# A one-layer decoder kernel: x on one DMA queue, and another order of work around the first products

## The chip, the cores and the metric

The kernel runs on one core of a Trainium2 chip. The metric is the device time of one execution in microseconds (us). A core has a matrix engine (PE, whose weight loads the profile lists as PEld), VectorE (DVE), ScalarE (ACT), GpSimd (POOL) and SyncE (SP), each with its own instruction stream; SP, ACT and POOL can issue DMA transfers. PE reads its operands from SBUF and writes into eight banks of PSUM.

## The reference

One layer of a decoder, batch 1, 512 tokens, width 1024, all in float32. What matters here is how it opens: a conditioning vector c gives a modulation (shift and scale, one row of weights for each), x is normalised and modulated, and multiplied by a wide input matrix.

```python
def layer(x, c, positions, ...):
    mod = silu(c) @ w_ada + b_ada               # shift, scale and gate of both sub-layers
    h   = rmsnorm(x, g1) * (1 + scale1) + shift1
    z   = h @ w_in                              # q, f, i, g of HGRN2; q, k, v, gates of NSA
    o   = concat(hgrn2(z...), nsa(z..., positions)) @ w_out
    x   = x + gate1 * o
    ...                                         # a second sub-layer: gated MLP with a causal convolution
```

The attention heads use rotary embeddings (sines and cosines of the positions), the recurrence uses a lower bound on its gate; both need small tables made from the inputs.

## The kernel before

**Precision.** Products of float32 values are made of three products in a reduced form: an operand is split into a high part (a cast, on ACT) and a low part (a subtraction, mostly on DVE), and high by high, high by low and low by high are summed in PSUM (`mm3`, `split`; lines L145, L146, L149 to L151).

**The opening.** x comes as four tiles of 128 tokens by 1024. For each, ACT squares and sums (`x_square`, L515), DVE and POOL make the inverse root (`x_rstd`, L349 and L350), DVE scales the tile (`x_scale`, L521), PE transposes it ("flips", `xn_flip`, L358: eight blocks of 128x128 a tile, four a half), and ACT or DVE copies the flipped blocks out of PSUM into `xnT` (`xn_out`, L363). The feature axis is cut into eight groups of 128, the turns k = 0 to 7. For each turn the modulation needs one shift and one scale column. For k = 0, 1, 2, 3 and 5 (`PROWS`) a row of products on PE makes it (`ada_first_row`, L376; its copy from PSUM by ACT is L381), then two transposes turn it into columns (`ada_cols`, L394, reduced on DVE in L395). For k = 4, 6 and 7 DVE sums the row (`sums_first`, L605 and L607) and PE adds up over partitions (L402). `h_scale` (L405, L406) makes `sh` and `a` of a column. The turn's input is `hT` = a * xnT + sh, in two parts: for k = 0 `h_first` (L413 to L416), for the others ACT makes the high part and the full value (L627) and DVE the low part (L634).

**The products.** A turn has three groups of four products on `accq` (L658: hT high by w high, hT high by w low, hT low by w high) and two triples on `accf` (L149 to L151). `wq` and `wf` are the split weights, from the raw tiles `raw` and `rawf`. The accumulators share PSUM banks with the tiles `ps` into which x is flipped.

**The tables.** `tables` makes, in small pieces, the gate's constants (`identr`, `onesr`, `bsc`, `lbv`, `fc`; L428 to L435), and the angles of the rotary embedding (L449 to L468).

**Order.** Up to the first products the order in which each engine works is the order in which the code is written. From there it is a string, `OPEN`: each letter takes one step of a part: P a group of products, R half a row on PE, s one sum on DVE, c a column, h a high part, l a low part, w a split of `wq`, f a split of `wf`, d the next load, t a piece of the tables, k a piece of later weights. A step that needs another forces it to be taken first (`reach`): P asks for `hT`'s low part and the weights of its turn, h for the column, c for the row. Within an engine nothing overtakes.

**Loads.** SP issues nearly all of them in the order of `LOADS`: the modulation's weights `ada` (two halves of 512 KB for each turn), `raw` (256 KB a turn) and `rawf`, behind the tiles of x, `vrow` (rows of small inputs) and `grow` (gains of heads). Tiles 1 and 2 of x and the constants `cb` are issued by ACT. Each SP transfer also waits for the landing of one that was issued eight transfers before it.

Of the kernel before, what the change touches and what calls it, by code (L numbers as in the profile page):

```python
# [10 lines left out]
F32R = mybir.dt.float32r  # L11
# [4 lines left out]
ALU = mybir.AluOpType  # L16
# [3 lines left out]
P = 128  # L20
# [8 lines left out]
HD = 64  # L29
# [2 lines left out]
WARM2 = 6  # L32
NPE = 3
AHD = 3
WARM4 = 4
PGP = 0
FLU = 1
FO = 1
# [7 lines left out]
GROUPS = tuple((k,) for k in range(8))  # L46
LOADS = "aqfaqcaaqfqaqaqfaifqaq"
PROWS = (0, 1, 2, 3, 5)
OPEN = ("tRwRPdPPcRRPPtRhcRhlRRPlfddPsdddcdPdwPddsPPPwshssdPPPdtdlPPPsddcwtddRfsdPhPssslcRwdhRPPsssPlsPsPPcfP",
        "sPsPhssssPsPwlcRhPPPtssPtPkwPtlPPPt")  # L50
EPOS = 1
VLAG = 1
# [52 lines left out]
def hybrid_layer_kernel(ctx: ExitStack, tc: tile.TileContext, d: dict, out: bass.AP, dbg=None):  # L105
    nc = tc.nc
    ve, sc, gp, pe, sp = nc.vector, nc.scalar, nc.gpsimd, nc.tensor, nc.sync
# [33 lines left out]
    def f32(ap):  # L141
        return ap.bitcast(F32)
# [20 lines left out]
    x_view = d["x"].rearrange("b (i p) c -> p (b i) c", p=P)  # L163
# [117 lines left out]
    xs = []  # L281
    for i in range(NT):
        xi = G([D], s="x")
        (sc if i in (1, 2) else sp).dma_start(xi, x_view[:, i, :])
        xs.append(xi)
        if i == 0:
            vrow = cst.tile([R_ALL, P], F32, name="vrow")
            sp.dma_start(vrow, d["rows"])
            grow = cst.tile([1, 4 * HD], F32, name="grow")
            sp.dma_start(grow, d["head_gains"])  # L290

    raw_f = []
    raw_q = []
# [17 lines left out]
    gains = cst.tile([P, 4, HD], F32, name="gains")  # L311
# [21 lines left out]
    ones = cst.tile([P, P], F32, name="ones")  # L333
# [20 lines left out]
    def xn_flip(i, half):  # L354
        ps = PS()
        for k in range(4):
            kk = half * 4 + k
            pe.transpose(ps[:, k * P:(k + 1) * P], xs[i][:, kk * P:(kk + 1) * P], ident)  # L358
        return ps.rearrange("p (e k t) -> p e k t", e=2, k=2)

    def xn_out(i, half, copy, ps, es=(0, 1)):
        for e in es:
            copy(xnT[2 * half + e][:, :, i * P:(i + 1) * P], ps[:, e])  # L363
# [23 lines left out]
    def ada_cols(g):  # L387
        t, one = arow.pop(g)
        m = len(GROUPS[g])
        if one is sel:  # L390
            c0 = 0 if m > 1 else 256 * (g % 2)
            turned = adcs[0][:, c0:c0 + m * 256]
            for b in range(2 * m):
                pe.transpose(turned[:, b * P:b * P + P], t[:, b % 2, b // 2 * P:b // 2 * P + P], ident)  # L394
            ve.tensor_reduce(acol[:, 2 * GROUPS[g][0]:2 * GROUPS[g][0] + 2 * m],  # L395
                             turned.rearrange("p (e g w) -> p e g w", e=2 * m, g=4)[:, :, :, 0], AX.X, ALU.add)
            ready[g] = acol
            return
        ready[g] = adcs[0]
        for n, k in enumerate(GROUPS[g]):  # L400
            for e in range(2):
                pe.matmul(adcs[0][:, 2 * k + e:2 * k + e + 1], t[:, e, n * P:(n + 1) * P], one, start=True, stop=True)  # L402

    def h_scale(k, adc):
        ve.tensor_tensor(sh1[:, k:k + 1], adc[:, 0:1], vt[:, k:k + 1], ALU.add)  # L405
        ve.scalar_tensor_tensor(a1[:, k:k + 1], adc[:, 1:2], bsc1[:, k:k + 1], vt[:, 48 + k:49 + k],  # L406
                                ALU.add, ALU.mult)

    def h_first(w):

        h = G([2, T], F32R, s="hT")
        t = TMP([P, T], tag="ht")
        ve.tensor_scalar(h[:, 0], xnT[0][:, 0], a1[:, 0:1], sh1[:, 0:1], ALU.mult, ALU.add)  # L413
        sc.activation(t, xnT[0][:, 0], AF.Identity, bias=sh1[:, 0:1], scale=a1[:, 0:1])
        ve.tensor_tensor(w[:, 1], raw_q[0], f32(w[:, 0]), ALU.subtract)
        ve.tensor_tensor(h[:, 1], t, f32(h[:, 0]), ALU.subtract)  # L416
        hT.append(h)
# [80 lines left out]
    def first_gates(k, eng):  # L498
        w = G([2, 2, 256], F32R, s="wf")
        split(w[:, 0], w[:, 1], raw_f[k // 2], eng)  # L500
        return w

    def warm_up(n):

        for _ in range(n):
            pe.matmul(warm, wrm[:, 0:P], wrm, start=True, stop=True)
# [6 lines left out]
    def x_square(i):  # L513
        sq = TMP([P, D], BF16, tag="sq")
        sc.activation(sq, xs[i], AF.Square, accum_out=ss1[:, i:i + 1])  # L515

    def x_rstd(i):
        rstd(rs1[:, i:i + 1], ss1[:, i:i + 1], 1.0 / D, EPS)

    def x_scale(i):  # L520
        ve.tensor_scalar(xs[i], xs[i], rs1[:, i:i + 1], None, ALU.mult)  # L521

    vps, gps = PS(), PS()
# [9 lines left out]
    pe.transpose(vps[:, 0:R_ALL], vrow, ident[0:R_ALL, 0:R_ALL])  # L533
    for _ in range(WARM2):
        pe.matmul(warm, wrm[:, 0:P], wrm, start=True, stop=True)
    sc.activation(csig, vps[:, R_C:R_C + KT], AF.Tanh, scale=0.5)
    x_rstd(0)
    ve.tensor_copy(vt, vps[:, 0:R_ALL])
    ve.tensor_scalar(bsc1, vt[:, 8:16], 1.0, None, ALU.add)
    x_scale(0)  # L540
    x_square(1)
    fl = {}
    for half in range(2):
        fl[0, half] = xn_flip(0, half)
    x_rstd(1)
    ve.scalar_tensor_tensor(cs, csig, 1.0, vt[:, R_C:R_C + KT], ALU.add, ALU.mult)
    ve.tensor_scalar(cs, cs, 0.5, None, ALU.mult)
    ve.tensor_copy(cs32, cs.unsqueeze(2).to_broadcast([P, KT, 32]))
    x_square(2)
    x_scale(1)  # L550
    x_rstd(2)
    for half in range(2):
        fl[1, half] = xn_flip(1, half)
    pe.matmul(gps[:, 0:4 * HD], ones[0:1], grow, start=True, stop=True)
    xn_out(0, 0, ve.tensor_copy, fl[0, 0])
    x_square(3)
    x_scale(2)
    xn_out(0, 1, sc.copy, fl[0, 1])
    xn_out(1, 0, sc.copy, fl[1, 0])
    for half in range(2):  # L560
        fl[2, half] = xn_flip(2, half)
    x_rstd(3)
    x_scale(3)
    for _ in ada_first_row(0):
        pass
    xn_out(2, 0, ve.tensor_copy, fl[2, 0])
    fl[3, 0] = xn_flip(3, 0)
    ada_cols(0)
    adc = ready[0][:, 0:2]
    xn_out(3, 0, ve.tensor_copy, fl[3, 0], (0,))  # L570
    fl[3, 1] = xn_flip(3, 1)
    w = G([2, 512], F32R, s="wq")
    sc.copy(w[:, 0], raw_q[0])
    h_scale(0, adc)
    h_first(w)
    xn_out(3, 0, ve.tensor_copy, fl[3, 0], (1,))
    xn_out(1, 1, sc.copy, fl[1, 1])
    xn_out(2, 1, sc.copy, fl[2, 1])
    xn_out(3, 1, sc.copy, fl[3, 1])
    ve.tensor_scalar(gains[:, 0], gps[:, 0:HD], HD ** -0.5, None, ALU.mult)  # L580
    ve.tensor_copy(gains[:, 1:4], gps[:, HD:4 * HD].rearrange("p (g c) -> p g c", g=3))
    wfk = first_gates(0, None)
    warm_up(WARM4)
    qw, fw = [w], [wfk]
    last = {}

# [95 lines left out]
    def advance(letter):  # L682
        name = same.get(letter, letter)
        last[name] = letter
        if next(opening[name], opening) is opening:
            return False
        made[name] += 1
        return True

    def reach(name, n):  # L690
        while made[name] < n:
            assert advance(name), name

# [1302 lines left out]
```

## Time and profile before

| | us |
|---|---|
| median of three runs | 678.23 (677.64 to 680.0) |
| the profiled execution | 678.53 |
| its span, first to last instruction | 676.7 |
| mean granted clock of PE | 0.999 |
| PE busy | 665.1 (98%) |
| DVE busy | 497.8 (74%) |
| ACT busy | 354.3 (52%) |
| POOL busy | 183.5 (27%) |

A row of the timeline gives the start, the busy time of the group, the engine, the line, the operation, the output and inputs, how many instructions, and in brackets how long the engine was idle ahead of it and what ended that. A row of stages gives the window and its length, the busy time and the number of instructions of PE, PEld, DVE, ACT and POOL, the granted clock of PE, the busy share of the DMA engines and their rate. Instructions on one engine overlap a little, so starts lie closer together than durations. Times are from the start of the span.

### The profile page before, as it was taken

What the parts mean: (1) busy time and instruction counts of PE and PEld (TensorE: products, weight loads), DVE (VectorE), ACT (ScalarE), POOL (GpSimd) and SP (SyncE); (2) the same over time, 40 slices, a digit from 0 to 9 for tenths busy, and PEclk for the clock granted to TensorE, in tenths of its full rate; (3) what the DMA queues carried; (4) which work ended last, traced back from release to release, by engine and by line L of the source; (5) the groups of instructions that cost most, each with busy time, mean ns of one, the idle gap of its engine ahead of it and who ended that gap; (6) DMA issues with size and microseconds to landing.
All of it is one profiled execution on the core that took longest, in us unless ns stands there. A gap on an engine that the chain in (4) does not pass through costs nothing.

```text
span 676.7 us, 11052 instructions
## 1 busy us (share of the span) xinstructions
PE 665.1 (98%) x4147; PEld 550.6 (81%) x4148; DVE 497.8 (74%) x971; ACT 354.3 (52%) x658; POOL 183.5 (27%) x185
## 2 busy tenths in 40 slices
PE   8999999999999999999999999999999999999996
PEld 4778898788888888888988888888888888888885
DVE  5788988979899879688746556655656558676997
ACT  5756447756687778245543434544433436464551
POOL 1006111000010100100036666747758645000000
PEclk9999999999999999999999999999999999999999
DMA  9936364576122316152258889999988946974662
GB/s 337 411 142 204 95 201 130 184 235 219 55 72 87 133 37 239 39 183 61 73 153 243 219 234 266 241 280 300 236 234 222 262 106 222 334 264 164 224 273 93
DMA packets 100731, 130.43 MB, mean 193 GB/s; under 512 B 6380, under 2 KB 67653, under 8 KB 100679
## 3 DMA queue, kind: packets, MB, share of 16 engines
q1 hardware_dynamic: 95735, 117.09, 51.4%
q0 software_dynamic: 4512, 11.54, 9.5%
q10 hardware_dynamic: 432, 1.12, 0.4%
q8 instruction: 32, 0.52, 0.3%
q14 instruction: 20, 0.16, 0.1%
HBM read 123.29 MB, written 29.50 MB: 226 GB/s over the span
## 4 chain that ended last, share of the span: by engine, by line
PE 81%; DVE 10%; ACT 5%; DMA 2%; issue 1%; ACTq 0%; SPq 0%; DVEq 0%
PE u L150 12%; PE u L149 12%; PE u L151 12%; PE dn L149 5%; PE dn L150 5%; PE dn L151 5%; PE accq L658 3%; PE oh L149 2%; PE oh L151 2%; PE oh L150 2%; PE oT L1127 2%; PE F L1098 2%; PE pT L149 2%; PE pT L151 2%; PE pT L150 2%
## 5 line engine op out<-in xcount | busy, mean ns | idle before, releaser
L146 DVE TENSOR_TENSOR wlo<-raw,whi 128x1024 fp32r<-128x1024 f32 (+1 forms) x67 | 90.9, 1358 | 100.5 <-ACT whi L145 100.4
L149 PE MATMUL u<-h2h,whi 128*128 128x512 f32 (+1 forms) x360 | 136.8, 380 | 0.0
L150 PE MATMUL u<-h2l,whi 128*128 128x512 f32 (+1 forms) x360 | 136.7, 380 | 0.0
L151 PE MATMUL u<-h2h,wlo 128*128 128x512 f32 (+1 forms) x360 | 136.7, 380 | 0.0
L145 ACT CAST whi<-raw 128x1024 fp32r<-128x1024 f32 (+1 forms) x67 | 68.8, 1028 | 80.9 <-PE u L150 74.3
L149 PEld LDWEIGHTS u<-h2h,whi 128*128 128x128 f32 x360 | 67.7, 188 | 12.9
L151 PEld LDWEIGHTS u<-h2h,wlo 128*128 128x128 f32 x360 | 67.7, 188 | 12.8
L150 PEld LDWEIGHTS u<-h2l,whi 128*128 128x128 f32 x360 | 67.7, 188 | 12.7
L350 POOL TENSOR_TENSOR hrs<-hrs,mhalf 128x4 f32<-128x4 f32 (+2 forms) x16 | 18.6, 1173 | 90.7 <-DVE hrs L349 88.7
L145 ACT CAST whi<-wd 128x1024 fp32r<-128x1024 f32 x20 | 21.1, 1055 | 40.5 <-PE dn L151 33.4
L1734 ACT ACTIVATE y<-y 128x512 f32<-128x512 f32 x22 | 13.9, 632 | 52.1 <-DVE y L1731 52.0
L1065 ACT ACTIVATE pt<-pt,mx 128x128 f32<-128x128 f32 (+3 forms) x64 | 35.9, 564 | 9.2 <-DVE mx L1049 8.1
L149 PE MATMUL pT<-hT,whi 128*128 128x512 f32 x96 | 38.3, 399 | 0.0
L150 PE MATMUL pT<-hT,whi 128*128 128x512 f32 x96 | 37.6, 391 | 0.0
L151 PE MATMUL pT<-hT,wlo 128*128 128x512 f32 x96 | 37.5, 391 | 0.0
L146 DVE TENSOR_TENSOR wlo<-wd,whi 128x1024 fp32r<-128x1024 f32 x20 | 25.5, 1275 | 14.3 <-ACT whi L145 14.3
L1730 DVE SCALAR_TENSOR_TENSOR y<-u,cv,y 128x511 f32<-128x511 f32 x44 | 32.6, 740 | 2.9 <-ACT y L1729 2.9
L150 PE MATMUL dn<-wlo,as 128*128 128x512 f32 x88 | 34.4, 391 | 0.1
L151 PE MATMUL dn<-whi,as 128*128 128x512 f32 x88 | 34.3, 389 | 0.0
L149 PE MATMUL dn<-whi,as 128*128 128x512 f32 x88 | 34.2, 389 | 0.0
L1731 DVE SCALAR_TENSOR_TENSOR y<-u,cv,y 128x510 f32<-128x510 f32 x44 | 32.9, 749 | 1.6
L1729 ACT ACTIVATE y<-u,cv 128x512 f32<-128x512 f32 x44 | 34.0, 773 | 0.0
(364 smaller groups left out, 1600.8 us busy)
## 6 DMA issues: line engine op xcount, KB each, us to landing
raw<-in_w_up SPq DMA_DIRECT2D x44, 512.0 KB, 6.1
aw<-in_w_ada SPq DMA_DIRECT2D x24, 512.0 KB, 4.0
ada<-in_ada_first SPq DMA_DIRECT2D x16, 512.0 KB, 8.1
raw<-in_w_in SPq DMA_DIRECT2D x7, 1024.0 KB, 5.1
wt<-in_w_down POOLq DMA_DIRECT2D x11, 512.0 KB, 8.6
wd<-in_w_down SPq DMA_DIRECT2D x11, 512.0 KB, 5.8
wt<-in_w_down SPq DMA_DIRECT2D x10, 512.0 KB, 6.5
wt<-in_w_down POOLq DMA_DIRECT2D x5, 1024.0 KB, 11.7
```

The costliest lines, as they stand in the source:

```text
L145: sc.copy(hi, src)
L146: (eng or ve).tensor_tensor(lo, src, f32(hi), ALU.subtract)
L149: pe.matmul(o, ah, bh, start=start, stop=False, skip_group_check=True)
L150: pe.matmul(o, ah, bl, start=False, stop=False, skip_group_check=True)
L151: pe.matmul(o, al, bh, start=False, stop=stop, skip_group_check=True)
L350: gp.tensor_tensor(o, o, mhalf[:, 0:n], ALU.pow)
L658: pe.matmul(accq[i], h[:, e, i * P:(i + 1) * P], w[:, f], start=(k + e + f == 0), stop=(e == 1 and k == KT - 1), skip_group_check=True)
L1065: sc.activation(pt[:, sl], pt[:, sl], AF.Exp, bias=mx[:, e:e + 1], scale=-1.0, accum_out=su[:, h % 2, e:e + 1])
L1729: sc.activation(y, u, AF.Identity, bias=cv[:, 132 + c:133 + c], scale=cv[:, 88 + c:89 + c])
L1730: ve.scalar_tensor_tensor(y[:, 1:], u[:, :T - 1], cv[:, 44 + c:45 + c], y[:, 1:], ALU.mult, ALU.add)
L1731: ve.scalar_tensor_tensor(y[:, 2:], u[:, :T - 2], cv[:, c:c + 1], y[:, 2:], ALU.mult, ALU.add)
L1734: sc.activation(y, y, AF.Silu)
```

## The change

All of it lies in the opening, about the first 30 us.

- All four tiles of x are issued by SP; `grow` goes to ACT's queue.
- The body up to the first products is written in another order: the squares of tiles 1 to 3 stand ahead of other work, the inverse roots of tiles 2 and 3 ahead of the scaling of tile 2; the gains are made early; the copies of tile 0 are all ACT's; row 0 of the modulation stands ahead of the flips of tile 2.
- Only the first half of tiles 2 and 3 is flipped ahead of the first products. The second halves follow the first group of products (`advance("P")`).
- The high part of turn 0's `wq` is cast by POOL in place of ACT.
- Five warm-up products in place of four, now ahead of `h_first`.
- `OPEN` has another first part: row 1 stands behind the first products, and the tables' pieces (t) behind the low part of turn 2.

```diff
-WARM4 = 4
+WARM4 = 5
-OPEN = ("tRwRPdPPcRRPPtRhcRhlRRPlfddPsdddcdPdwPddsPPPwshssd...
+OPEN = ("wPRRRPcPPhlPRRRPchPltRRRPPtfddsdddcddwddsPPwshssd...
-        (sc if i in (1, 2) else sp).dma_start(xi, x_view[:, i, :])
+        sp.dma_start(xi, x_view[:, i, :])
-            sp.dma_start(grow, d["head_gains"])
+            sc.dma_start(grow, d["head_gains"])
...
     for _ in ada_first_row(0):
         pass
-    xn_out(2, 0, ve.tensor_copy, fl[2, 0])
-    fl[3, 0] = xn_flip(3, 0)
+    w = G([2, 512], F32R, s="wq")
+    gp.tensor_copy(w[:, 0], raw_q[0])
+    xn_out(0, 1, sc.copy, fl[0, 1])
+    fl[2, 0] = xn_flip(2, 0)
+    xn_out(2, 0, ve.tensor_copy, fl[2, 0], (0,))
     ada_cols(0)
-    adc = ready[0][:, 0:2]
+    fl[3, 0] = xn_flip(3, 0)
     xn_out(3, 0, ve.tensor_copy, fl[3, 0], (0,))
-    fl[3, 1] = xn_flip(3, 1)
-    w = G([2, 512], F32R, s="wq")
-    sc.copy(w[:, 0], raw_q[0])
+    adc = ready[0][:, 0:2]
     h_scale(0, adc)
-    h_first(w)
-    xn_out(3, 0, ve.tensor_copy, fl[3, 0], (1,))
+    warm_up(WARM4)
     xn_out(1, 1, sc.copy, fl[1, 1])
-    xn_out(2, 1, sc.copy, fl[2, 1])
-    xn_out(3, 1, sc.copy, fl[3, 1])
+    h_first(w)
+    for i in (2, 3):
+        xn_out(i, 0, sc.copy, fl[i, 0], (1,))
...
+    advance("P")
+    for i in (2, 3):
+        fl[i, 1] = xn_flip(i, 1)
+        xn_out(i, 1, sc.copy, fl[i, 1])
     for row in OPEN:
```

Behind the edits the code's lines are three lower: L627 becomes L624, L634 L631, L658 L655, L605 L602, L607 L604; from the 700s on they are one higher.

On SP's queue before, with the names of the tiles (x_79, x_85, x_87 and x_89 are tiles 0 to 3):

```order
1 L284 DMA x_79<-in_x 128x1024
2 L288 DMA vrow<-in_rows 112x128
3 L290 DMA grow<-in_head_gains 1x256
4 L284 DMA x_89<-in_x 128x1024
5 L277 DMA ada_93<-in_ada_first 128x1024
6 L277 DMA ada_95<-in_ada_first 128x1024
```

and now:

```order
1 L284 DMA x_79<-in_x 128x1024
2 L288 DMA vrow<-in_rows 112x128
3 L284 DMA x_85<-in_x 128x1024
4 L284 DMA x_87<-in_x 128x1024
5 L284 DMA x_89<-in_x 128x1024
6 L277 DMA ada_93<-in_ada_first 128x1024
```

Tiles 1 and 2 now stand ahead of tile 3 and of the modulation's weights in one queue.

On PE before, from row 0 of the modulation to the first products (ps are flipped halves of x, adc the column, wrm the warm-up):

```order
41 L376 MATMUL warm_110<-ada_93,cs_157 32x256 x4
42 L376 MATMUL warm_110<-ada_95,cs_157 32x256 x4
43 L358 MATMUL ps_247<-cb,x_89 128x128 x4
44 L394 MATMUL adc_152<-cb,row_243 128x128 x2
45 L358 MATMUL ps_256<-cb,x_89 128x128 x4
```

and now, with the second halves of tiles 2 and 3 behind the first group of products:

```order
39 L376 MATMUL warm_110<-ada_93,cs_157 32x256 x4
40 L376 MATMUL warm_110<-ada_95,cs_157 32x256 x4
41 L358 MATMUL ps_239<-cb,x_87 128x128 x4
42 L394 MATMUL adc_152<-cb,row_233 128x128 x2
43 L358 MATMUL ps_248<-cb,x_89 128x128 x4
```
```order
57 L655 MATMUL accq_149<-wq_235,hT_263 128x512
58 L358 MATMUL ps_278<-cb,x_87 128x128 x4
59 L358 MATMUL ps_285<-cb,x_89 128x128 x4
60 L655 MATMUL accq_146<-wq_235,hT_263 128x512
61 L655 MATMUL accq_147<-wq_235,hT_263 128x512
62 L655 MATMUL accq_148<-wq_235,hT_263 128x512
63 L655 MATMUL accq_149<-wq_235,hT_263 128x512
64 L376 MATMUL warm_110<-ada_101,cs_157 32x256 x4
65 L376 MATMUL warm_110<-ada_103,cs_157 32x256 x4
```

Row 1 (ada_101, ada_103) stood ahead of the first products and now stands behind two groups of them.

On DVE before, from the split of wf to the weights of turn 2 (wq_422):

```order
34 L146 TENSOR_TENSOR wf_280<-rawf_99,wf_280 128x512
35 L430 TENSOR_SCALAR bsc_136<-vt 128x8
36 L431 TENSOR_TENSOR lbv<-vt 128x4
...
44 L466 TENSOR_SCALAR rnd<-rnd 128x32
45 L468 SCALAR_TENSOR_TENSOR ang<-rnd,ang 128x32 x4
...
52 L634 TENSOR_TENSOR hT_371<-xnT_128,hT_371 128x512
53 L146 TENSOR_TENSOR wf_388<-rawf_99,wf_388 128x512
54 L607 TENSOR_SCALAR rows_400<-ada_392,cs 128x256
55 L395 TENSOR_REDUCE acol<-adc_152 128x2
56 L146 TENSOR_TENSOR wq_422<-raw_97,wq_422 128x512
```

and now (hT_356 and wq_429 are turn 2's):

```order
39 L631 TENSOR_TENSOR hT_356<-xnT_128,hT_356 128x512
40 L430 TENSOR_SCALAR bsc_136<-vt 128x8
41 L431 TENSOR_TENSOR lbv<-vt 128x4
...
47 L466 TENSOR_SCALAR rnd<-rnd 128x32
48 L468 SCALAR_TENSOR_TENSOR ang<-rnd,ang 128x32 x4
49 L146 TENSOR_TENSOR wf_403<-rawf_99,wf_403 128x512
50 L604 TENSOR_SCALAR rows_411<-ada_407,cs 128x256
51 L395 TENSOR_REDUCE acol<-adc_152 128x2
52 L146 TENSOR_TENSOR wq_429<-raw_97,wq_429 128x512
```

The nine rows of tables moved from behind the first split of wf to between the low part of turn 2 and its weights.

More of the change, by code (lines that the diff above doesn't have):

```diff
@@ L48 @@
 PROWS = (0, 1, 2, 3, 5)
-OPEN = ("tRwRPdPPcRRPPtRhcRhlRRPlfddPsdddcdPdwPddsPPPwshssdPPPdtdlPPPsddcwtddRfsdPhPssslcRwdhRPPsssPlsPsPPcfP",
+OPEN = ("wPRRRPcPPhlPRRRPchPltRRRPPtfddsdddcddwddsPPwshssdPPPdtdlPPPsddcwtddRfsdPhPssslcRwdhRPPsssPlsPsPPcfP",
         "sPsPhssssPsPwlcRhPPPtssPtPkwPtlPPPt")
@@ L535, in hybrid_layer_kernel @@
         pe.matmul(warm, wrm[:, 0:P], wrm, start=True, stop=True)
+    x_rstd(0)
     sc.activation(csig, vps[:, R_C:R_C + KT], AF.Tanh, scale=0.5)
-    x_rstd(0)
+    x_square(1)
     ve.tensor_copy(vt, vps[:, 0:R_ALL])
@@ L540, in hybrid_layer_kernel @@
     x_scale(0)
-    x_square(1)
     fl = {}
@@ L544, in hybrid_layer_kernel @@
         fl[0, half] = xn_flip(0, half)
-    x_rstd(1)
+    pe.matmul(gps[:, 0:4 * HD], ones[0:1], grow, start=True, stop=True)
+    x_square(2)
     ve.scalar_tensor_tensor(cs, csig, 1.0, vt[:, R_C:R_C + KT], ALU.add, ALU.mult)
     ve.tensor_scalar(cs, cs, 0.5, None, ALU.mult)
+    x_rstd(1)
     ve.tensor_copy(cs32, cs.unsqueeze(2).to_broadcast([P, KT, 32]))
-    x_square(2)
+    x_square(3)
     x_scale(1)
-    x_rstd(2)
     for half in range(2):
         fl[1, half] = xn_flip(1, half)
-    pe.matmul(gps[:, 0:4 * HD], ones[0:1], grow, start=True, stop=True)
-    xn_out(0, 0, ve.tensor_copy, fl[0, 0])
-    x_square(3)
+    x_rstd(2)
+    ve.tensor_scalar(gains[:, 0], gps[:, 0:HD], HD ** -0.5, None, ALU.mult)
+    ve.tensor_copy(gains[:, 1:4], gps[:, HD:4 * HD].rearrange("p (g c) -> p g c", g=3))
+    xn_out(0, 0, sc.copy, fl[0, 0])
+    x_rstd(3)
     x_scale(2)
-    xn_out(0, 1, sc.copy, fl[0, 1])
     xn_out(1, 0, sc.copy, fl[1, 0])
-    for half in range(2):
-        fl[2, half] = xn_flip(2, half)
-    x_rstd(3)
     x_scale(3)
@@ L565, in hybrid_layer_kernel @@
         pass
-    xn_out(2, 0, ve.tensor_copy, fl[2, 0])
+    w = G([2, 512], F32R, s="wq")
[3 more added lines that the diff above has]
+    xn_out(2, 0, ve.tensor_copy, fl[2, 0], (0,))
+    ada_cols(0)
     fl[3, 0] = xn_flip(3, 0)
-    ada_cols(0)
+    xn_out(3, 0, ve.tensor_copy, fl[3, 0], (0,))
     adc = ready[0][:, 0:2]
-    xn_out(3, 0, ve.tensor_copy, fl[3, 0], (0,))
-    fl[3, 1] = xn_flip(3, 1)
-    w = G([2, 512], F32R, s="wq")
-    sc.copy(w[:, 0], raw_q[0])
     h_scale(0, adc)
+    warm_up(WARM4)
+    xn_out(1, 1, sc.copy, fl[1, 1])
     h_first(w)
-    xn_out(3, 0, ve.tensor_copy, fl[3, 0], (1,))
-    xn_out(1, 1, sc.copy, fl[1, 1])
-    xn_out(2, 1, sc.copy, fl[2, 1])
-    xn_out(3, 1, sc.copy, fl[3, 1])
-    ve.tensor_scalar(gains[:, 0], gps[:, 0:HD], HD ** -0.5, None, ALU.mult)
-    ve.tensor_copy(gains[:, 1:4], gps[:, HD:4 * HD].rearrange("p (g c) -> p g c", g=3))
+    for i in (2, 3):
+        xn_out(i, 0, sc.copy, fl[i, 0], (1,))
     wfk = first_gates(0, None)
-    warm_up(WARM4)
     qw, fw = [w], [wfk]
```

## Prediction

> **What bounds the kernel now.** I read the page first (busy times, then the chain that ended last), then a table of stages, then the DMA issues and the timeline of the opening, which is all the change touches.
>
> ```profile
> PE 665.1 (98%) x4147; PEld 550.6 (81%) x4148; DVE 497.8 (74%) x971; ACT 354.3 (52%) x658; POOL 183.5 (27%) x185
> PE 81%; DVE 10%; ACT 5%; DMA 2%; issue 1%; ACTq 0%; SPq 0%; DVEq 0%
> ```
>
> TensorE is busy 98% of the span and carries 81% of the chain. By stage (columns: window and length, busy us of PE, PEld, DVE, ACT, POOL, granted clock, DMA share, GB/s):
>
> ```profile
> 0.00:5.00 5.00, 3.40 (x9) 1.21 (x10) 1.10 (x9) 1.84 (x2) 0.20 (x4) 1.00 0.63 219
> 5.00:10.00 5.00, 4.55 (x25) 2.74 (x24) 2.68 (x10) 2.69 (x6) 1.13 (x2) 1.00 1.01 356
> 10.00:15.00 5.00, 3.99 (x37) 2.53 (x36) 3.07 (x9) 3.26 (x10) 1.32 (x3) 1.00 1.03 404
> 20.00:25.00 5.00, 4.65 (x45) 2.51 (x44) 3.35 (x18) 2.97 (x6) 0.00 (x0) 1.00 1.05 406
> 25.00:30.00 5.00, 5.00 (x23) 4.08 (x24) 4.05 (x10) 2.99 (x6) 0.00 (x0) 1.00 1.03 410
> 30.00:35.00 5.00, 5.00 (x24) 4.14 (x23) 4.69 (x17) 4.66 (x8) 0.00 (x0) 1.00 1.03 411
> 300.00:600.00 300.00, 300.00 (x1410) 251.70 (x1409) 185.35 (x225) 134.37 (x189) 149.88 (x133) 1.00 0.78 223
> ```
>
> The clock is 1.00 in every row. Behind the opening PE has no gap (300.00 of 300.00), so whatever the opening gains or loses by its third turn of products (k=2, from where all engines do the same work in the same order in both kernels) is carried to the end. DMA share is 1.0 from 5 us on; VectorE has free time from 20 to 25 (3.35 of 5) and almost none from 30 to 35 (4.69).
>
> **The first products, the part that gains.** The transfers (KB each, median us from issue to landing), and the chain before the first product:
>
> ```profile
> x<-in_x SPq DMA_DIRECT2D x2, 512.0 KB, 3.7
> x<-in_x ACTq DMA_DIRECT2D x2, 512.0 KB, 7.4
> raw<-in_w_in SPq DMA_DIRECT2D x8, 256.0 KB, 8.0
> ```
> ```profile
> 9.11 1.06 ACT L515 ACTIVATE sq<-x 128x1024 bf16<-128x1024 f32 x1 [1.63 <-DMA x<-in_x]
> 12.94 1.07 PE L376 MATMUL warm<-ada,cs 128*32 128x256 f32 x16
> 14.08 0.37 ACT L381 COPY row<-warm 128x256 f32<-128x256 f32 x1 [1.71 <-PE warm L376]
> 14.51 0.44 PE L394 MATMUL adc<-cb,row 128*128 128x128 f32 x2
> 15.07 0.41 DVE L363 COPY xnT<-ps 128x256 f32<-128x256 f32 x1
> 15.43 0.81 PE L506 MATMUL warm<-wrm 128*128 128x512 bf16 x3
> 15.46 0.21 DVE L406 SCALAR_TENSOR_TENSOR a<-acol,bsc,vt 128x1 f32<-128x1 f32 x1
> 15.79 0.55 DVE L413 TENSOR_SCALAR hT<-xnT,a,sh 128x512 fp32r<-128x512 f32 x1
> 16.18 1.07 PE L376 MATMUL warm<-ada,cs 128*32 128x256 f32 x16
> 17.17 0.30 PEld L658 LDWEIGHTS accq<-wq,hT 128*128 128x128 f32 x2 [0.41 <-ACT xnT L363]
> 17.18 3.15 PE L658 MATMUL accq<-wq,hT 128*128 128x512 f32 x12
> ```
>
> A tile of x on ACT's queue took 7.4 us and one on SP's 3.7; tile 2 came at 9.1, and ACT waited 1.63 us for it. Row 0 of the modulation ran behind its flips and ended at 14.01 (12.94 + 1.07). With all of x first on SP's queue, a tile takes 1.47 us (0.524 MB at 356 GB/s), so the tiles land near 4.4, 5.9, 7.4 and 8.9. But the bytes in the stream stay the same, so row 0's second half of weights is then what is waited for: 3.27 MB (x, constants, rows, two ada halves) less 1.10 by 5 us and 1.78 by 10 leave 0.39 MB, hence 11.0 at 404 GB/s, and up to 12.3 if what is queued behind shares the rate; I take 11.65. (SP issues one more DMA ahead of ada, 0.4 us in a queue that waits for landings anyway; ACT issues two fewer.)
>
> The Trainium skill, "DMA: Bandwidth & Descriptors", under "Issuing engines are not separate DMA queues" and "Queues, rings and completion order", says that SP's and ACT's transfers run on the same 16 engines, which alternate between the two rings packet by packet, so that a second issuer saves only issue time. By that rule tile 2 comes earlier only because ada stands behind it, and ada itself no earlier than before; the 7.4 against 3.7 us agrees, and what it makes of the time is the second rival's.
>
> Row 0 ends half its 1.07 later plus a start: R = 11.65 + 0.6 = 12.25 (11.6 to 12.9). From R: one half flip 0.55, adc 0.44, one half flip 0.55, the copy of xnT 0.41, scalings and a to 2.3, hT 0.55: first product T1 = R + 2.85 = 15.1 (14.45 to 15.75), against 17.18. Row 1 (1.07) and two half flips, which before stood ahead of it, now stand behind it. The fifth warm-up product is 0.27 (0.81 for three) and ends by R + 2.9, so it costs 0.05 at most. The cast of w on POOL has no row; the nearest are
>
> ```profile
> L1481 POOL TENSOR_TENSOR aw<-aw 128x512 f32<-128x512 f32 x16 | 24.2, 1510 | 1.3
> L1475 POOL MEMSET aw<- 128x512 f32 x2 | 1.1, 528 | 0.0
> ```
>
> 0.53 to 1.51 us; a copy reads one operand and I take 1.1, between. The raw tile issued at 5.0 lands near 13.0, so the cast ends by 14.5 even at the upper end; it is covered by the flips and hT until T1, except against the earliest T1 (0.1).
>
> **From there to k=2.** The rows of before:
>
> ```profile
> 19.38 0.16 DVE L430 TENSOR_SCALAR bsc<-vt 128x8 f32<-128x8 f32 x1
> 20.15 0.17 DVE L435 TENSOR_SCALAR fc2n<-fc 128x4 f32<-128x4 f32 x1
> 20.68 0.44 PE L394 MATMUL adc<-cb,row 128*128 128x128 f32 x2 [0.35 <-ACT row L381]
> 21.23 0.18 DVE L450 TENSOR_TENSOR ang<-vt,cb 128x32 f32<-128x32 f32 x1
> 21.88 0.87 DVE L468 SCALAR_TENSOR_TENSOR ang<-rnd,ang 128x32 f32<-128x32 f32 x4
> 22.74 0.21 DVE L406 SCALAR_TENSOR_TENSOR a<-acol,bsc,vt 128x1 f32<-128x1 f32 x1
> 22.99 0.81 ACT L627 ACTIVATE hT<-xnT,sh,a 128x512 fp32r<-128x512 f32 x1 [0.43 <-DVE a L406]
> 23.84 0.81 ACT L627 ACTIVATE xnT<-xnT,sh,a 128x512 f32<-128x512 f32 x1
> 24.68 0.69 DVE L634 TENSOR_TENSOR hT<-xnT,hT 128x512 fp32r<-128x512 f32 x1 [0.23 <-ACT xnT L627]
> 27.02 0.69 DVE L146 TENSOR_TENSOR wf<-rawf,wf 128x512 fp32r<-128x512 f32 x1
> 27.97 0.68 DVE L146 TENSOR_TENSOR wq<-raw,wq 128x512 fp32r<-128x512 f32 x1
> 29.32 2.88 PE L658 MATMUL accq<-wq,hT 128*128 128x512 f32 x12
> ```
>
> PE's own work: 29.32 - 17.18 = 12.14, less the 0.35 of idle, plus row 1 (1.07) and the flips (two halves at 0.55) make 13.96. By PE alone k=2 would start at 15.1 + 13.96 = 29.06, or 0.26 early (0.9 early to 0.4 late). So even in full the gain is small: most of what the first product wins is paid back by work moved behind it.
>
> The other limit is VectorE's and ACT's order. The small tables (L430 to L435, L450 to L468) ran before at 19.38 to 20.32 and 21.23 to 22.75, while column 1 was awaited. Now they stand behind the low part of hT of k=2 and ahead of wf's and wq's low parts. Counted from T1, by PE's order: four products 0.9 (twelve took 2.88), flips 1.1, four products 0.9 and row 1 1.07 (3.97), four products (4.87), adc 0.38 (5.25); scalings 0.65 (0.72 above from adc's end, 14.95, to a's, with a copy between; 5.9); hT high 0.82 (6.7); then four products, row 2, four products and adc 3.27 (10.0); scalings (10.65), hT and xnT of k=2 at 0.82 each (12.3), the low part 0.69 (13.0). Then the tables, as long as before: 0.94 (19.38 to 20.32, with ACT's lbv between), 1.52 (21.23 to 22.75), and 0.1 to start (15.55). From wf's low part to wq's end there were 28.65 - 27.02 = 1.63: wq's low part is ready at T1 + 17.2 = 32.3. It is the second factor of k=2's second group of four products, which before began at 29.32 + 0.9 = 30.22. So PE's stream is late there by 2.1.
>
> Does VectorE lose more on the way to k=4? It is late by 32.3 - 28.65 = 3.65 against PE's 2.1. What is wanted next of it:
>
> ```profile
> 33.10 1.52 DVE L605 SCALAR_TENSOR_TENSOR rows<-ada,cs,rows 128x256 f32<-128x256 f32 x3
> 36.12 0.50 PE L402 MATMUL adc<-ones,rows 128*128 128x1 f32 x4
> 39.84 0.44 PE L394 MATMUL adc<-cb,row 128*128 128x128 f32 x2 [0.49 <-ACT row L381]
> ```
>
> The rows for column 4 were done at 34.62 and used at 36.12, a slack of 1.5 against 3.65 - 2.1 = 1.55; and ahead of k=4 PE waited 0.49 for a row on ACT already. So 0 to 0.3 more is lost; I take 0.1. Sum: 2.1 + 0.1 = +2.2. The ends: T1 at 14.45 gives 31.65 - 30.22 = +1.4; T1 at 15.75 gives +2.7 and 0.3, +3.0. Two of ACT's casts (identr, onesr) also moved; they lie beside VectorE's low part and tables.
>
> The profiled execution took 678.53 (span 676.7 and 1.8 round it), 0.3 above the median of 678.23. From it the sum is 680.7; from the median 680.4, which I give, its own range 679.6 to 681.2. The measurement of this kernel can tell about 0.3%, or 2.03 us.
>
> **The rivals.**
> - The tables are covered. VectorE has 1.65 free in 20 to 25 and may catch up if k=1's columns come earlier than I count. Then PE's own sum decides: -0.26, about 678.0 (677.3 to 678.6). It decides once wq's low part is there 2.4 us sooner, at T1 + 14.8. Against it: an engine doesn't overtake in its order, and the tables alone are 2.5 us.
> - One queue brings ada no earlier (the rule above): T1 = 15.75, +2.7 to +3.0, 681.1. For it: the stream was full from 5 us on. Against it: before, ada shared the rate with the tiles on ACT's queue.
> - Faster, the other sign: ada lands at 11.0 (T1 = 14.45), the tables are covered, and the wait for the copies of xnT at the first products (0.41) goes as well: k=2 at 28.0, -1.3; the 0.49 before k=4 goes with it, -1.8; with 0.3 less between R and T1 than I count, -2.1, or 676.1. It takes wq's low part at T1 + 14.4 or before.
> - POOL's cast is slower than any row of this shape, 3 us: T1 = 16.0, +3.1, 681.3.
>
> **How the numbers follow.** The forecast has 0.47 (of it 0.31 above +2.03 us, 0.16 below); covered tables 0.24 (within 0.3%); ada no earlier 0.14 (0.12 slower, 0.02 within); faster 0.08; POOL 0.07 (slower 0.06). That makes slower 0.49, within 0.3% 0.43, faster 0.08. The range goes from the covered case's low end, 677.3, to 681.6, a little above the two slow rivals; it leaves out the faster case and some of the tails.
>
> **What would show it.** Right: tile 2's square starts before 8.5, row 0 ends at 11.6 to 12.9, first product at 14.5 to 15.8; VectorE's L450 to L468 lie directly ahead of wf's and wq's low parts and PE waits for DVE wq ahead of k=2's second group; k=4 starts near 42.2 against 40.03. Wrong: no such wait and k=2 before 29.5 (covered), or a first product past 16.

## The result and the profile after

The changed kernel takes 682.36 us (median of six, 681.84 to 683.67) against 678.23 before: a ratio of 1.0062 with a 95% interval of 1.0044 to 1.0079, or 4.1 us slower (3.0 to 5.4). Its profiled execution took 682.44, span 680.4, against 678.53 and 676.7. Forecast was 680.4, within 677.3 to 681.6: the side was right, the size too small. Three executions on record, of 1287, 1706 and 2939 us, are slow ones and stand in none of the ratios.

The stages of the changed kernel, in the columns of the table of before:

```profile
5.00:10.00 5.00, 4.78 (x20) 2.45 (x18) 2.17 (x9) 2.75 (x7) 1.11 (x2) 1.00 1.00 339
10.00:15.00 5.00, 3.89 (x36) 2.50 (x38) 3.25 (x10) 3.85 (x13) 2.39 (x4) 1.00 1.03 401
20.00:25.00 5.00, 4.96 (x36) 3.07 (x32) 1.41 (x5) 2.01 (x3) 0.00 (x0) 1.00 1.04 405
30.00:35.00 5.00, 3.32 (x13) 2.28 (x14) 4.76 (x20) 1.74 (x5) 0.00 (x0) 1.00 0.66 262
300.00:600.00 300.00, 300.00 (x1410) 251.69 (x1409) 183.92 (x225) 132.74 (x188) 147.17 (x133) 1.00 0.78 220
```

The loss shows most in one row: from 30 to 35 us PE is busy 3.32 where it had been 5.00, while VectorE is full (4.76). From 20 to 25 VectorE has 1.41 where it had 3.35: the work that filled its gap there stands later. The DMA share of 30 to 35 fell to 0.66. From 300 to 600 us PE is as full as before (300.00).

The timeline of its first products:

```profile
7.69 1.06 ACT L515 ACTIVATE sq<-x 128x1024 bf16<-128x1024 f32 x1 [1.25 <-DMA x<-in_x]
8.99 1.06 ACT L515 ACTIVATE sq<-x 128x1024 bf16<-128x1024 f32 x1
12.72 0.64 PE L376 MATMUL warm<-ada,cs 128*32 128x256 f32 x8 [0.55 <-DMA ada<-in_ada_first]
13.41 0.61 POOL L566 CAST wq<-raw 128x512 fp32r<-128x512 f32 x1 [0.76 <-DMA raw<-in_w_in]
16.18 1.16 PE L655 MATMUL accq<-wq,hT 128*128 128x512 f32 x4 [0.38 <-DVE hT L413]
```

Tile 1 is squared at 7.69 instead of 6.34, tile 2 at 8.99 instead of 9.11. Row 0's second half waits for its weights until 12.72, and the first product is at 16.18: 1.0 earlier than before, where 2.1 was forecast. And around k=2 and ahead of k=4:

```profile
28.73 0.69 DVE L631 TENSOR_TENSOR hT<-xnT,hT 128x512 fp32r<-128x512 f32 x1 [1.74 <-ACT xnT L624]
29.34 0.17 DVE L430 TENSOR_SCALAR bsc<-vt 128x8 f32<-128x8 f32 x1
30.85 0.87 DVE L468 SCALAR_TENSOR_TENSOR ang<-rnd,ang 128x32 f32<-128x32 f32 x4
31.16 1.20 PE L655 MATMUL accq<-wq,hT 128*128 128x512 f32 x4 [0.60 <-ACT wq L145]
31.64 0.69 DVE L146 TENSOR_TENSOR wf<-rawf,wf 128x512 fp32r<-128x512 f32 x1
32.57 0.69 DVE L146 TENSOR_TENSOR wq<-raw,wq 128x512 fp32r<-128x512 f32 x1
33.31 2.14 PE L655 MATMUL accq<-wq,hT 128*128 128x512 f32 x8 [0.96 <-DVE wq L146]
43.38 0.44 PE L394 MATMUL adc<-cb,row 128*128 128x128 f32 x2 [0.76 <-ACT row L381]
43.57 3.02 PE L655 MATMUL accq<-wq,hT 128*128 128x512 f32 x12
```

The tables run from 29.34 to 31.72, directly ahead of the low parts of wf and wq, and PE waits 0.60 for ACT's cast of wq and 0.96 for DVE's low part. k=2's second group starts at 33.31 (30.22 before, which is 29.32 and four products at 0.9; +3.09) and k=4 at 43.57 (40.03, +3.54).

### The profile page after: what moved, and what is told of

It is laid out like the page before. It is cut to its first block, busy times and chain, and to the rows that moved or that the text cites. A ratio compares the mean times of both kernels' runs of the same rounds, so it can differ in the third digit from the quotient of the medians.

```text
span 680.4 us, 11054 instructions
## 1 busy us (share of the span) xinstructions
PE 666.8 (98%) x4148; PEld 550.4 (81%) x4149; DVE 494.7 (73%) x967; ACT 356.0 (52%) x661; POOL 182.0 (27%) x186
## 4 chain that ended last, share of the span: by engine, by line
PE 77%; DVE 11%; ACT 5%; DMA 4%; issue 2%; POOL 0%; SPq 0%; DVEq 0%; ACTq 0%
PE u L151 12%; PE u L149 12%; PE u L150 12%; PE dn L151 5%; PE dn L150 5%; PE dn L149 5%; PE accq L655 2%; DMA ada<-in_ada_first 2%; PE oT L1128 2%; PE F L1099 2%; PE pT L149 2%; PE pT L150 2%; PE pT L151 2%; PE oh L149 2%; PE oh L151 2%; PE oh L150 2%
## 5 line engine op out<-in xcount | busy, mean ns | idle before, releaser
L146 DVE TENSOR_TENSOR wlo<-raw,whi 128x1024 fp32r<-128x1024 f32 (+1 forms) x67 | 89.3, 1333 | 102.2 <-ACT whi L145 102.1
```

Source lines behind the costliest of these rows:

```text
L146: (eng or ve).tensor_tensor(lo, src, f32(hi), ALU.subtract)
```

## The experiments

The start times that the runs are judged by, in us (k=2 and k=4 are the first product of the turn). Where the starts are left out, the granted clock in that profile was below 1.00 somewhere between 10 and 20 us, so they can't be set beside the others' (more on it below). Ratios are against the kernel before on the same chip, with 95% intervals; between two runs of the table they compare better than medians do, since the kernel before itself had medians of 678.04 to 678.41 on the chips that were used.

| kernel | first product | k=2 | k=4 | median | ratio |
|---|---|---|---|---|---|
| before | 17.18 | 29.32 | 40.03 | 678.23 | |
| changed | 16.18 | 31.16 | 43.57 | 682.36 | 1.0062 (1.0044 to 1.0079) |
| tables_early | 16.11 | 29.97 | 41.36 | 679.64 | 1.0022 (1.0013 to 1.0031) |
| queues_back | 15.64 | 30.59 | 42.99 | 681.23 | 1.0046 (1.0034 to 1.0058) |
| early_and_queues | 15.65 | 29.51 | 40.90 | 679.04 | 1.0010 (1.0002 to 1.0019) |
| one_queue | | | | 678.42 | 1.0012 (1.0003 to 1.0021) |
| tables_late | | | | 678.55 | 1.0007 (0.9998 to 1.0016) |
| one_queue_warm | 17.36 | 29.51 | 40.23 | 678.49 | 1.0003 (0.9995 to 1.0012) |
| swap23 | 17.39 | 29.54 | 40.25 | 678.89 | 1.0005 (0.9996 to 1.0015) |
| swap23_row1 | | | | 679.71 | 1.0020 (1.0010 to 1.0031) |
| fill2 | 15.70 | 28.68 | 40.07 | 678.95 | 1.0013 (1.0004 to 1.0022) |
| fill3 | 15.77 | 28.42 | 39.13 | 678.05 | 0.9995 (0.9986 to 1.0004) |
| ada_ahead | | | | 685.29 | 1.0100 (1.0081 to 1.0119) |
| w_on_act | | | | 682.90 | 1.0063 (1.0048 to 1.0078) |

**tables_early**

```diff
-OPEN = ("wPRRRPcPPhlPRRRPchPltRRRPPtfdds...
+OPEN = ("twPRRRPcPPhtlPRRRPchPlRRRPPfdds...
```

> The changed kernel with the tables' two pieces where they were before (the first ahead of wq of turn 1, the second behind column 1); the rest of the change stays. Theory A, the tables stand on the way to wq's low part of turn 2: that part is ready by 31.0 instead of 33.3, PE's second group of k=2 starts at 31.0, and the time falls by 2.3 us to about 680.1 (679.6 to 680.6). Rival, the wait at k=2 is ACT's (row copy and casts come late anyway): only the 0.6 us that PE waits for ACT's cast moves, 681.8 or no change at 682.4.

```profile
29.97 3.25 PE L655 MATMUL accq<-wq,hT 128*128 128x512 f32 x12
41.36 3.00 PE L655 MATMUL accq<-wq,hT 128*128 128x512 f32 x12
```

Theory A holds. The first product is where it was (16.11), PE's waits for wq are gone, k=2 starts 13.86 behind the first product, and the time is 2.7 us lower: two thirds of the whole loss are two letters of the string.

**queues_back**

```diff
-        sp.dma_start(xi, x_view[:, i, :])
+        (sc if i in (1, 2) else sp).dma_start(xi, x_view[:, i, :])
-            sc.dma_start(grow, d["head_gains"])
+            sp.dma_start(grow, d["head_gains"])
```

> The changed kernel with x and the gains on the queues of before (tiles 1 and 2 and not the gains on ACT); the rest of the change stays. Theory B, one queue made tile 1 and the second half of the modulation's weights late: tile 1 is squared at 6.3 again instead of 7.7, row 0's second half starts near 12.3 instead of 12.7, the first product near 15.75 instead of 16.2, time 682.0. Rival, the queues don't matter because the bytes are the same: first product 16.2, 682.4. Third, tile 2 is late again and with it the half flip behind row 0: first product 16.5 or more, 682.8.

```profile
6.06 1.06 ACT L515 ACTIVATE sq<-x 128x1024 bf16<-128x1024 f32 x1 [0.22 <-DMA x<-in_x]
12.17 0.64 PE L376 MATMUL warm<-ada,cs 128*32 128x256 f32 x8 [0.61 <-DMA ada<-in_ada_first]
15.64 1.16 PE L655 MATMUL accq<-wq,hT 128*128 128x512 f32 x4 [0.38 <-DVE hT L413]
```

Theory B holds: with two queues tile 1 is squared at 6.06, row 0's second half starts at 12.17 and the first product comes at 15.64. The trace gives 0.58 at k=4; the medians differ by 1.1, with the intervals overlapping. With the tables early, the same step (tables_early to early_and_queues) gives 0.46 at k=4 and 0.6 by the medians. So the one queue cost about half a microsecond; the time, 681.23, is below the 682.0 that was expected.

**one_queue** (the same lines, turned round, in the kernel before)

> The kernel before with only the queues changed (all tiles of x on SP, the gains on ACT). Theory B: tile 1 is squared at 7.7 instead of 6.3, tile 2 at 9.0 as before, so flips of tile 2 and row 0 stay where they are (row 0 from 12.9), first product 17.2, time 678.2 within 0.4. Rival, as the prediction counted (a tile takes 1.47 us in one queue, tile 2 comes at 7.4): first product earlier by 0.7 to 1.2, time 677.0 to 677.5. Third, the tile that comes late delays row 0: 678.9.

The median is 0.4 higher (0.2 to 1.4 by the interval), so the rival that the forecast rested on, a gain, is excluded. Tile 1 was squared at 7.54 and tile 2 at 8.82, as in the changed kernel. Three of the twelve executions lie at 679.8 or above; in the one of them that was profiled the clock was down, so how much of the 0.4 is the queue stays open.

**tables_late** (the letters t of the kernel before moved behind the second l)

> The kernel before with only the tables' two pieces moved behind the low part of turn 2, as the change has them. Theory A: that low part ends at 26.9, tables 2.5 us and wf, rows, column and wq 1.6 us behind it, so wq's low part is ready at 31.1 against 30.2 where PE's second group of k=2 starts: +0.9 there, and 0 to 0.3 more on the way to k=4, time 679.1 to 679.4. Rival, they are covered by PE's work before k=2 also there: 678.2.

+0.5, with an interval from -0.1 to 1.1: less than forecast and not told apart from nothing. Its trace has one wait for DVE at k=2:

```profile
31.02 2.11 PE L658 MATMUL accq<-wq,hT 128*128 128x512 f32 x8 [0.35 <-DVE wq L146]
```

In the order of before, the low part of turn 2 ends 9.75 behind the first product (26.93 less 17.18), in the changed order 13.2 (29.42 less 16.18). The same move of the tables therefore costs 2.7 in the one and 0.5 in the other: row 1, the half flips and the order of the letters make columns 1 and 2 late (column 2's transposes start 9.9 behind the first product and not 6.4), and the tables stood behind them.

**early_and_queues** (tables_early and queues_back together)

> The changed kernel with the tables where they were before and the queues of before; the rest of the change (half flips and row 1 behind the first products, order of the opening, POOL's cast) stays. If the two losses add up, first product at 15.6, k=2 at 15.6 + 13.9 = 29.5, k=4 near 40.9 against 40.0 before, time 678.9 (678.5 to 679.3). Rival, the moved flips and row cost nothing and the earlier first product remains as a gain: 676.5 to 677.7.

```profile
29.51 3.25 PE L655 MATMUL accq<-wq,hT 128*128 128x512 f32 x12
40.90 3.02 PE L655 MATMUL accq<-wq,hT 128*128 128x512 f32 x12
```

k=4 at 40.90 and 679.04, both as forecast. What is left of the change, with the first product 1.5 earlier, is still 0.7 us slower than before.

**w_on_act** (the changed kernel with `sc.copy` for `gp.tensor_copy`)

> The changed kernel with the high part of turn 0's wq cast by ACT again, in the place in the code where POOL has it. POOL's cast took 0.61 us and ended at 14.0, two us ahead of the first product at 16.2, so on POOL it is covered. Theory, on ACT it takes 0.62 ahead of four copies, hT's full value still starts near 15.5: no change, 682.4 within 0.4. Rival, the copies for the accumulators' banks come 0.6 later and hold the first products: 683.0.

A ratio of 1.0063 against 1.0062: no change is seen. It was four executions, the interval (3.3 to 5.3 us above before) holds the rival's 683.0 too, and the clock was down in the profile, so the run alone doesn't decide. The changed kernel's own trace says more: POOL's cast (0.61) ended at 14.02, two us ahead of the first product, which waited for hT.

**ada_ahead**

```diff
+        if i == 3:
+            load_ada()
         sp.dma_start(xi, x_view[:, i, :])
...
-    for _ in range(5):
+    loaded["a"] = 1
+    for _ in range(4):
```

> The changed kernel with both halves of turn 0's modulation weights issued ahead of tile 3 of x; nothing else. It tells what sets a landing on the one queue. Theory D, read off the changed kernel (7.7, 9.0, 10.2, 11.5, 12.7 for tiles 1 to 3 and the two halves): behind the second transfer one of 512 KB lands each 1.25 us by its place, so the halves land near 10.2 and 11.5 and tile 3 at 12.7. Rival, the count of the prediction (a transfer lands when the bytes ahead of it and its own have moved): second half at 10.0 or before. Third, what stands behind does not matter and all land as before: 12.7 for the second half. The time itself should rise by 1 to 2 us by theory D, since ACT squares tile 3 ahead of its copies and tile 3 comes 2.5 us later: 683.4 to 684.5.

Each SP transfer waits for one landing, so on this queue issues and squares mark the landings (tile 1, tile 2, first half, second half, tile 3):

```profile
8.06 1.06 ACT L518 ACTIVATE sq<-x 128x1024 bf16<-128x1024 f32 x1 [1.62 <-DMA x<-in_x]
9.37 1.06 ACT L518 ACTIVATE sq<-x 128x1024 bf16<-128x1024 f32 x1 [0.16 <-DMA x<-in_x]
10.61 0.33 SPq L317 DMA_DIRECT2D cb<-in_consts  x1
11.85 2.94 SPq L277 DMA_DIRECT2D ada<-in_ada_first  x4
13.11 1.06 ACT L518 ACTIVATE sq<-x 128x1024 bf16<-128x1024 f32 x1 [2.59 <-DMA x<-in_x]
```

Behind tile 1, one place in the queue is worth 1.24 to 1.31 us, as theory D has it; everything is 0.4 later than it said because tile 1 is. The weights came 0.85 earlier by moving up one place and tile 3 2.9 later. The rival count (10.0) is excluded. The time rose from the changed kernel by 2.9 by the medians and 2.6 by the ratios, more than forecast; PE then also waits 2.2 us for tile 2's scaling, which stands behind the root of tile 3 on DVE, and the clock was at 0.65 over 16 to 20 us, so that the first four products took 2.02 in place of 1.16.

**swap23** (the kernel before with tile 2 on SP and tile 3 on ACT)

> The kernel before with tile 2 of x on SP's queue and tile 3 on ACT's. Theory, what tile 2 loses on ACT's queue (9.1 us against 5.8 for tile 3) can be given to the tile that is needed last: flips of tile 2 at 10.3 instead of 11.9, row 0 bound by its weights near 12.3 and ended by 13.1 instead of 14.0, first product earlier by 0.4 (row 1's weights land at 16.2 and row 1 is ahead of it), 677.6. Rival, PE or the weights of row 0 bind as before: 678.04. Third, tile 3 late holds the flips of it and hT: 678.5.

```profile
9.32 1.06 ACT L515 ACTIVATE sq<-x 128x1024 bf16<-128x1024 f32 x1 [1.36 <-DMA x<-in_x]
```

My theory fell. Tile 2 on SP's queue was squared at 9.32, no earlier than on ACT's (9.11). The 5.8 for the other tile was its issue at 2.02 and the 3.7 of SP's row, and that 3.7 is tile 0's (issued at 0.74, squared at 4.44), whose transfer was the first; no row of the kernel before has a landing of tile 3. The third tile came between 8.4 and 9.4 in every arrangement of queues that was run.

**swap23_row1** (as swap23, `twPRR` for `tRwRP`)

> As swap23, with row 1 of the modulation behind the first group of four products instead of ahead of it (letters twPRR in place of tRwRP); tables, half flips and the rest as before. Theory, then nothing ahead of the first product waits for row 1's weights: first product near 16.0, k=2 at 16.0 + 12.1 + 1.1 - 0.35 = 28.85 against 29.3, 677.4 to 677.7. Rival, row 1 behind the products makes column 1 and with it turn 1 late, as the change did: 678.5 to 679.5.

679.71 is nearest to the rival's range of 678.5 to 679.5, and above it. In its profile the clock was down, and half of its twelve executions lie above 680, so how much of this is row 1 and how much the clock stays open.

**one_queue_warm** (one_queue with `warm_up(8)` ahead of the flips of tile 1)

> The kernel before with all tiles of x on SP (as in one_queue) and eight more warm-up products ahead of the flips of tile 1, where one_queue left PE idle for 1.9 us. Theory C, that idle time is what lets the granted clock fall to a half near 12 to 15 us in some executions of one_queue (680.5, 680.3 and 679.8 among its twelve): no execution is above 679.3 and the median is 678.0 to 678.3. Rival, the clock falls for another reason: about three in ten executions stay at 679.8 or more, median 678.4. The eight products are 1.7 us and may themselves cost 0 to 0.2.

The highest is 679.68 and the second 679.19, against 680.49, 680.28 and 679.84 in one_queue; the median is 678.49, the ratio 1.0003 in place of 1.0012, with overlapping intervals. The profile shows the clock at 1.00 throughout. This fits theory C, but its bound of 679.3 was passed once, eleven executions do not settle it, and the kernel before, run beside them without the long gap, had 680.98 and 680.10 among its 35. tables_late speaks against the theory: its clock fell with no idle stretch of PE above 0.9 us (last section).

**fill2 and fill3.** Of early_and_queues' waiting time ahead of the first product, both use 1.1 us for the second half flips and leave the warm-up products out; fill3 has the opening's letters of before with row 1 behind the first group.

```diff
     ada_cols(0)
+    fl[2, 1] = xn_flip(2, 1)
     fl[3, 0] = xn_flip(3, 0)
     xn_out(3, 0, ve.tensor_copy, fl[3, 0], (0,))
+    fl[3, 1] = xn_flip(3, 1)
     adc = ready[0][:, 0:2]
     h_scale(0, adc)
-    warm_up(WARM4)
     xn_out(1, 1, sc.copy, fl[1, 1])
+    xn_out(2, 0, sc.copy, fl[2, 0], (1,))
+    xn_out(2, 1, sc.copy, fl[2, 1])
+    xn_out(3, 0, sc.copy, fl[3, 0], (1,))
+    xn_out(3, 1, sc.copy, fl[3, 1])
     h_first(w)
-    for i in (2, 3):
-        xn_out(i, 0, sc.copy, fl[i, 0], (1,))
...
-    for i in (2, 3):
-        fl[i, 1] = xn_flip(i, 1)
-        xn_out(i, 1, sc.copy, fl[i, 1])
```

> As early_and_queues, but PE flips the second halves of tiles 2 and 3 ahead of the first products, in the time in which early_and_queues ran five warm-up products and waited (1.5 us between its last flip and first product); there are no warm-up products at that place, and ACT copies those halves before it makes hT's full value. Theory, PE's own sum decides: first product at 15.7 as there, k=2 1.1 us earlier, near 28.4 against 29.3 before; some of it is given back where turn 2's wq waits for DVE (0.4 in early_and_queues, up to 1 here), time 677.6 to 678.2, faster than the kernel before or equal. Rival, ACT's copies now stand ahead of the first products (their PSUM banks) and hold them by 0.7 or more: 678.7 or above.

> As fill2, with the opening's letters of the kernel before, only row 1 behind the first group of products. Theory, columns 1 and 2 come as in the kernel before, so nothing is given back at turn 2: k=2 at 15.7 + 13.2 = 28.9, k=4 at 39.6 against 40.0, time 677.6 to 678.0. Rival, as for fill2: 678.7 or above.

The first products of k=0, k=2 and k=4 in fill3:

```profile
15.77 1.16 PE L658 MATMUL accq<-wq,hT 128*128 128x512 f32 x4 [1.02 <-ACT xnT L363]
28.42 2.88 PE L658 MATMUL accq<-wq,hT 128*128 128x512 f32 x12
39.13 3.00 PE L658 MATMUL accq<-wq,hT 128*128 128x512 f32 x12
```

fill2 gives its 0.6 at k=2 back before k=4 (40.07), so it is not faster. Its 678.95 lies in the rival's range, but the rival's mechanism is not there: PE did wait 1.02 for ACT's copies, and the first product still came at 15.70, against 15.65 in early_and_queues. fill3 differs from it in the letters alone, so it is the change's letters once more. fill3 keeps 0.9 to k=4, and its profiled execution took 677.45 against 678.53. Its median is 0.2 below the kernel's before, with an interval from 0.9 below to 0.3 above: at least as good as both kernels, and not shown to be faster.

## Why the prediction missed

- **The step that failed: the landing of row 0's weights.** I counted the bytes ahead of it (3.27 MB) and divided by the rate, "hence 11.0 [...] and up to 12.3". It landed at 12.7, so row 0 ended at 13.36 and the first product came at 16.18 and not at 15.1: 1.1 of the 2.0 us that are missing, and outside of its own bounds (a first product past 16 was named as a sign of being wrong). The windows of the changed kernel say it in numbers: by 12.7 the stream had moved 1.02 + 1.70 + 2.7 x 0.401 = 3.8 MB, so 0.5 MB of what stood behind had moved already. The same for tile 1: it landed at 7.7 when 1.9 MB had moved, of which 1.2 were its own and what stood ahead. Here, then, a transfer on the full queue was complete one to one and a half places (0.5 to 0.75 MB) later than the bytes say; from there on one landed each 1.25 us. That place in the queue orders the landings, ada_ahead showed; that transfers behind run beside those ahead is what the sums say, and was not tested by itself. The Trainium skill, "DMA: Bandwidth & Descriptors", "Two DMAs through the same engine are not ordered", says that within a queue the pieces of transfers start in order and are then pipelined; the 0.5 MB agrees. I had drawn on neighbouring sections and made it a rival with 0.14, that one queue brings the weights no earlier. That rival had the direction: row 0's second half started at 12.72 on one queue and at 12.17 on two (queues_back; 11.55 to 11.87 in the three other runs with two queues and this order). Its first product, 15.75, was still too early. The rival with a slow cast on POOL was nearer in numbers (16.0 and 681.3), and by luck, since the cast took 0.61 and not 3 us.
- **What stood behind that landing.** The sum R + 2.85 has no term for the scaling of tile 3 on DVE. It came out here because row 0 was later still. In early_and_queues row 0 ended at 12.19 (11.55 + 0.64), near the 12.25 of the forecast, and the first product was at 15.65, not at 15.1, because PE waited for that scaling:

```profile
12.23 1.18 DVE L521 TENSOR_SCALAR x<-x,rs 128x1024 f32<-128x1024 f32 x1 [0.44 <-POOL rs L350]
12.26 0.61 POOL L566 CAST wq<-raw 128x512 fp32r<-128x512 f32 x1
13.56 0.63 PE L358 MATMUL ps<-cb,x 128*128 128x128 f32 x4 [0.44 <-DVE x L521]
```

  The scaling took 1.18 there and 0.75 in the changed kernel (12.69, ahead of POOL's cast at 13.41). So weights in time would have saved only part of the 1.1, in the changed kernel some 0.6 by an estimate from its rows: tile 3's flip ran at 14.12, and its scaling had ended at 13.44.
- **Tile 2.** I expected it at 7.4; it came at 8.99. The change of queues made tile 1 1.35 later and tile 2 0.1 earlier. The 7.4 us of ACT's queue and the 3.7 of SP's were those of tile 2 and of tile 0, so they compared the first transfer with a later one and not two queues: on SP's queue tile 1 took 6.0 (issued at 1.65, squared at 7.69). So they say nothing for or against the rule that the prediction cites.
- **From row 0 to the first product** 2.85 were forecast and 2.82 passed (13.36 to 16.18).
- **The tables.** wq's low part for k=2 at T1 + 17.2 was forecast; the second group started 17.13 behind the first product, with PE's wait of 0.96 for it. This part of the mechanism was right, and tables_early shows it. I didn't count that ACT's cast of wq would be late as well (0.60), but it lies within the same 17.1.
- **PE's own sum**, 13.96 from the first product to k=2, is 13.86 in tables_early: the work moved behind the first product is paid for in full, but for 0.1.
- **From k=2 to k=4** I took 0.1 and it was 0.45 (3.09 to 3.54). 0.17 of it is there by the first product of k=3 (36.66 against 33.40). 0.27 is the wait for ACT's copy of row 5, 0.76 and not 0.49: ACT came to it only behind `xnT`, and to that late because DVE made `a` of column 4 at 41.16 (36.73 before, 4.43 later). The slack that I took for column 4's rows was nearly right (PE's loads waited 0.17 for them); the column's `a` had none. Now, and in the kernel before:

```profile
42.26 0.81 ACT L624 ACTIVATE xnT<-xnT,sh,a 128x512 f32<-128x512 f32 x1
42.98 0.35 ACT L381 COPY row<-warm 128x256 f32<-128x256 f32 x1
39.42 0.37 ACT L381 COPY row<-warm 128x256 f32<-128x256 f32 x1 [0.78 <-PE warm L376]
```

  SP's queue, whose issues I had put at nothing, was held up too: its transfer of other weights waited for DVE's splits, and two halves of `ada` stood behind it. Before (first row) and after:

```profile
SPq L207 <- DVE rows L605: 2.9, 1, 2.9
SPq L207 <- DVE wq L146: 6.6, 1, 6.6
```

  This fits the hole in the DMA share at 30 to 35 us. PE lost nothing by it up to k=4: from row 5's first half to its second there were 2.15 us (39.83 to 41.98), and 2.16 before.
- **The warm-up product and POOL's cast** cost nothing in the changed kernel, as said (0.61 for the cast against 1.1 taken). That holds as long as the cast doesn't meet DVE's scaling of a tile: in early_and_queues they began 0.03 apart and the scaling took 1.18 in place of 0.75; in fill2 and fill3 the cast came second and took 1.09 and 0.98 in place of 0.61.
- **The rest**, 4.1 by the medians against 3.54 at k=4, is within the interval (3.0 to 5.4). The two profiled executions differ by 3.9, their spans by 3.7, and at 57 us the products are still 3.55 late; no run looked for what is left.

## What to carry to other kernels

An engine that executes in order has its free time where it waits, not on average: work that fills such a gap is free, and the same work one step later, behind the thing that was awaited, can be on the path (2.7 us here; in the order of before, where the awaited columns come earlier, at most 1.1). Before counting on a transfer, take its landing from a neighbour's place in the queue and not from bytes over rate, and look for the next thing that would be waited for if it came in time. And when the first product is brought forward by moving work behind it, the sum of the matrix engine's work up to the next fixed point is what decides: here 1.0 to 1.5 us earlier left nothing.

## What the hardware showed that I had not expected

The matrix engine's granted clock fell to a half for some 3.5 us in the opening of some executions. The stages of 8 to 12 and 12 to 16 us of one_queue, of one_queue_warm, of the kernel before, and of tables_late:

```profile
8.00:12.00 4.00, 2.12 (x15) 1.41 (x13) 3.00 (x10) 3.78 (x10) 1.18 (x3) 1.00 0.99 376
12.00:16.00 4.00, 4.00 (x29) 2.39 (x28) 1.42 (x3) 0.65 (x4) 0.71 (x2) 0.57 1.04 410
8.00:12.00 4.00, 4.00 (x26) 2.44 (x23) 3.00 (x10) 3.79 (x10) 1.12 (x2) 1.00 1.01 374
12.00:16.00 4.00, 4.00 (x38) 2.69 (x38) 2.14 (x8) 1.28 (x5) 0.77 (x2) 1.00 1.04 410
8.00:12.00 4.00, 2.59 (x19) 1.78 (x18) 2.68 (x7) 2.89 (x8) 0.90 (x2) 1.00 1.00 342
12.00:16.00 4.00, 3.95 (x37) 2.61 (x38) 2.33 (x8) 1.49 (x5) 0.77 (x2) 1.00 1.05 414
8.00:12.00 4.00, 2.71 (x19) 1.91 (x17) 2.32 (x6) 3.27 (x8) 1.12 (x3) 0.97 0.98 342
12.00:16.00 4.00, 4.00 (x31) 2.40 (x30) 1.57 (x5) 0.89 (x2) 0.20 (x1) 0.60 1.06 420
```

In one_queue PE was busy 2.12 of the 4 us ahead of the fall, with no idle stretch over 1.9 us, and then row 0 took 1.94 us instead of 1.07. tables_late is the kernel before, unchanged on PE up to the first products, and PE was as busy in it (2.71 against 2.59); its profiled execution lost the clock, with no idle stretch over 0.9 us, and that of the kernel before kept it. So the same opening can go either way, and what decides stays open. The Trainium skill, "TensorE: Matmul & The Clock Gate", Part 1, gives an idle window of about 3.4 us as the condition for half rate; here gaps of 1.9 us and less between short bursts were enough in these two profiles. A fall cost more than its waits: one_queue's profiled execution took 680.49 against its median of 678.42, and in w_on_act the first product came at 17.05 in place of 16.18. A single profile may not show it.
